# A decoder layer on one core: indexer queries for tokens 128 to 511 only, and the forgetting bias as causal strips loaded per query block

## The chip, the core and the metric

The kernel runs on one core of a Trainium2 chip. The metric is the device time of one execution in microseconds (us); lower is better. The kernel before takes 1047.29 us (median of 3 runs, 1047.10 to 1047.31).

The core has five engines that run their own instruction streams in order and wait for each other through semaphores: PE (TensorE, matrix products into PSUM), DVE (VectorE), ACT (ScalarE), POOL (GpSimd) and SP (SyncE, which here only issues DMAs). In the profile PEld is PE's loading of weights, which runs beside its matmuls.

## The reference, cut to what matters

One decoder layer for 512 tokens of width 1024: a half-step feed-forward block, a mixing stage, a second half-step feed-forward block. The mixing stage projects the normalised tokens `h` and runs two attentions of 8 heads of width 64 each, in blocks of 128 queries. The change touches two places in it.

```
# branch A, forgetting attention: log_f per token and head
cum = cumsum(log_f over tokens)
logits[t,s] = q_t.k_s / 8 + cum[t] - cum[s]       for s <= t, else -1e30
o_A = softmax(logits) @ v
...
# branch B, sparse attention: an indexer scores the keys, top 128 are kept
score[t,s] = sum over 8 heads of w[t,h] * relu(q_idx[t,h].k_idx[s] / 8)
score = where(s <= t, score, -1e30);  sel = top_k(score, 128)
o_B = softmax over sel of (q.k / 8 + rel_bias[bucket(t - s)]) @ v
```

Queries 0 to 127 can see at most 128 keys, so top-k keeps them all and their scores decide nothing. A softmax does not change when a number that depends on the query alone, such as `cum[t]`, is left out of its logits.

## The kernel before, in words

Everything is held with tokens or features on the 128 partitions; T = 512 tokens are NT = 4 blocks of 128. Matrix products are in split form: each operand is a high part plus a low part (`wh`, `wl` for weights, `xh`, `xl` for activations), and `mm3` (lines 154 to 157) issues three matmuls per product. A matmul of 128x512 reads 512 columns of the moving operand.

**Who sets the order.** PE's order is the order in which the program is written. All other engines and the DMA queues are ordered by a scheduler that places instructions by estimated times. SP issues nearly all loads in one in-order queue: the weight chunks (`load_w`, line 143, 512 KB each, three raw buffers `ra`, `rb`, `rc`), the key halves `kh`, `kl` (line 1300) and the bias tiles (line 1306).

**The filler.** The projections of the mixing stage are `units` (small columns `s`, indexer queries `iq0` to `iq3`, gates `ga`, keys, queries and values of branch A `fk`, `fq`, `fv`, queries of branch B `dq`, and so on), run by a generator. `prod.run(us)` runs filler steps until a budget is used up; each step yields its own estimate, `MM` = 0.64 for one feature-major step of three 128x512 matmuls, MM/2 for a token-major step of three 128x256 matmuls. `prod.finish(n)` runs units to the end whatever the budget.

**The indexer** (lines 1210 to 1226, 354 to 381 us). Units `iq0` to `iq3` each make the queries of two indexer heads (24 matmuls `ps_f`), and `stack_split` turns each into two tiles `st`: ACT copies the high part (line 916), DVE subtracts for the low part (line 917), tokens 0 to 511. For each of 8 heads and query blocks i = 1, 2, 3 there are two score matmuls `ps_ix` of 128x128(i+1), then ACT's relu (line 1220) and DVE's weighted sum into `sc` (line 1224). Block 0 is never scored. The score matmuls alternate between two PSUM tags of two buffers each. Filler of 0.5 us budget lies ahead of each.

**Top-k** (lines 1183 to 1193). 16 rounds of a maximum (MAX8, line 1187) and a replacement (MATCH_REPLACE8, line 1189) on each of three `sc` tiles, and three last comparisons (line 1192): 99 steps on DVE. They are handed out by `topk_run`: 1.25 steps per 0.64 us of filler after the indexer until the unit `fq0` is done, then for 30 further rounds, and after that two steps per attention block. DVE also splits the weights (line 150), the queries and keys (lines 920, 890).

**The running sums.** `forget()` makes `cum` on PE and DVE, `ncum` = -`cum` on DVE (line 1174), transposes `cum`, and stores it in DRAM as `cum_rows` (line 1181).

**The attention loop** (lines 1374 to 1400, 432 to 645 us). Heads g = 0 to 7 are branch A, 8 to 15 branch B. For each head s = 0 to 3 handles query block i = 3 - s. `softmax_block` (from line 1231):

- POOL makes the bias tile `b` for the block. For g < 8 that is a TENSOR_SCALAR `b<-cb,ncum` (line 1312: `cb` is one row of `cum_rows` read into all 128 partitions, and `ncum` a number per query) and an AFFINE_SELECT on the diagonal 128x128 (line 1313), which puts BIG above the diagonal. For g >= 8 it is one TENSOR_TENSOR (line 1316).
- PE makes the scores `ps_qk` (two PSUM buffers), DVE adds `b` and takes the minimum of each row in one instruction (line 1238, `p<-ps_qk,b`), ACT takes the exponential with its row sum (line 1240), DVE the reciprocal `rs` (line 1241), POOL the scaling `p<-p,rs` (line 1242).

`value_step` follows one head later: PE transposes the four `p` tiles (`pt`, line 1249), ACT and DVE split the result into `ph`, `pl` (lines 1253, 1254), and PE multiplies them with the values (`po`, lines 1259 and 1260). `get_bias(g + 1)` issues the DMA for the next head's `cb` at s = 0; `cb` has two buffers. Filler runs inside every block.

Of the kernel before, what the change touches and what calls it, by code (L numbers as in the profile page):

```python
# [12 lines left out]
F32 = mybir.dt.float32  # L13
# [42 lines left out]
def tile_hybrid_layer(ctx: ExitStack, tc: tile.TileContext, a: dict):  # L56
# [812 lines left out]
    with (tc.tile_pool(name="mix", bufs=1) as mp, ExitStack() as att_ctx,  # L869
# [6 lines left out]
        sg = at.tile([P, NT, S_W - 128], F32, name="sg")  # L876
# [4 lines left out]
        cum = at.tile([P, NT, H], F32, name="cum")  # L881
        ncum = at.tile([P, NT, H], F32, name="ncum")
# [26 lines left out]
        def stack_split(ps, g, nm):  # L909

            out = []
            for hf in range(2):
                own, oth = slice(hf * DH, hf * DH + DH), slice(DH - hf * DH, P - hf * DH)
                st = at.tile([P, T], F32R, tag=nm[hf], bufs=2, name="st")
                if g is None:
                    S.copy(st[own], ps[own])
                    V.tensor_sub(st[oth], ps[own], st[own].bitcast(F32))
                else:
                    S.mul(st[own], ps[own], g[own])
                    V.scalar_tensor_tensor(st[oth], ps[own], g[own], st[own].bitcast(F32),  # L920
                                           op0=OP.mult, op1=OP.subtract)
                out.append(st)
            return out
# [9 lines left out]
        def fm_proj(w, moving, kn, done):  # L933
            def run():
                ps = acc_tile("ps_f")
                wh, wl = w()
                for k in range(kn):
                    mm3(ps, wh[:, k], wl[:, k], moving[0][k], moving[1][k], k == 0, k == kn - 1)
                    if k < kn - 1:
                        yield MM  # L940
                done(ps)
                yield MM
            return run
# [128 lines left out]
        for c in range(4):  # L1072
            unit(f"iq{c}", fm_proj(weight(a["w_iq"][c], KD, P), (xh, xl), KD, iq_done))
# [71 lines left out]
        def forget():  # L1145
# [26 lines left out]
            PE.matmul(pc[:, :NT * H], ones, before.rearrange("p t h -> p (t h)"), start=False, stop=True)  # L1172
            V.tensor_copy(cum, pc[:, :NT * H].rearrange("p (t h) -> p t h", t=NT))
            V.tensor_scalar(ncum, cum, -1.0, None, op0=OP.mult)
# [128 lines left out]

        def get_bias(g):
            cb = at.tile([P, T], F32, tag="cb", bufs=2, name="cb")
            nc.sync.dma_start(cb, cum_rows[g:g + 1, :].to_broadcast([P, T]) if g < H else a["rel"][g - H])

            def bias(i):
                n = P * (i + 1)
                b = tmp_tile("b")  # L1310
                if g < H:
                    G.tensor_scalar(b[:, :n], cb[:, :n], 1.0, ncum[:, i, g:g + 1], op0=OP.mult, op1=OP.add)
                    G.affine_select(out=b[:, i * P:n], in_=b[:, i * P:n], compare_op=OP.is_ge, fill=BIG, base=0,
                                    pattern=[[-1, P]], channel_multiplier=1)
                else:
                    G.tensor_sub(b[:, :n], sc[i] if i else cpos, cb[:, T - n:T])
                return b[:, :n]
            return bias
# [6 lines left out]
        for step in range(30):  # L1325
# [8 lines left out]
            if step == 24:  # L1334
                nb = get_bias(0)
# [38 lines left out]
        for g in range(2 * H):  # L1374
            q, k, bias = nq, nk, nb
            probs[g] = [None] * NT
            st = [small.tile([P, NT], F32, tag=nm, name=nm) for nm in ("mn", "rs")]
            for s in range(NT):
# [6 lines left out]
                if g + 1 < 2 * H:  # L1385
                    if s == 0:
                        nb = get_bias(g + 1)
                    if s == 0 and g % 2:
                        nk = get_k(g + 1)
                    if s == 1 and g % 2:  # L1390
                        nq = get_q(g + 1)
# [131 lines left out]
```

## Time and profile before

| | |
|---|---|
| median of 3 runs | 1047.29 us (1047.10 to 1047.31) |
| the profiled execution, its own time | 1047.09 us |
| span of its trace | 1045.4 us |
| mean granted TensorE clock | 0.999 |
| PE busy | 1033.6 us, 99% of the span |
| DVE busy | 852.9 us, 82% |
| ACT busy | 669.0 us, 64% |
| POOL busy | 259.3 us, 25% |
| DMA | 142.66 MB, mean 136 GB/s |

How to read it: the span runs from the first to the last instruction in the trace; 1.7 us of the execution lie around it. A matmul's busy time overlaps with its neighbours', so the pace of a run of matmuls is read from their starts. In a timeline, a number in brackets is the engine's idle time just before, and behind the arrow stands what ended it. "waited for" rows give the total, the number of times and the longest.

### The profile page before, as it was taken

How to read it: one execution, taken by the hardware profiler on the slowest of the kernel's cores; microseconds unless marked ns; L12 is line 12 of the kernel's file. 1: busy time of each engine (PE TensorE's matmuls, PEld its weight loads, DVE VectorE, ACT ScalarE, POOL GpSimd, SP SyncE). 2: the span in 40 equal slices, each digit the busy share in tenths (PEclk: the TensorE clock that was granted, in tenths of full speed). 3: DMA queues.
4: the chain of work that ended last, by engine and by line, in shares of the span. 5: the costliest groups of instructions: out<-in, count | busy, mean ns of one | idle time of the engine just before them, and what ended most of it. 6: DMA issues, size and time to landing. Idle time of an engine off the chain costs nothing.

```text
span 1045.4 us, 19485 instructions
## 1 busy us (share of the span) xinstructions
PE 1033.6 (99%) x7424; PEld 962.6 (92%) x7424; DVE 852.9 (82%) x1405; ACT 669.0 (64%) x1118; POOL 259.3 (25%) x324
## 2 busy tenths in 40 slices
PE   9999999999999999999999999999999999999998
PEld 8889999999999898989977788888889999999998
DVE  6897888897989689977778765854887888988887
ACT  6547765865777766567867665433735865775773
POOL 1100111120121024386977653000100210111111
PEclk9999999999999999999999999999999999999999
DMA  7444765666567358633324321532553666567554
GB/s 259 105 151 120 158 165 129 152 163 173 120 150 182 91 147 192 188 104 90 92 69 117 117 70 51 158 131 74 131 168 90 152 147 182 127 160 190 135 127 131
DMA packets 57341, 142.66 MB, mean 136 GB/s; under 512 B 6424, under 2 KB 15768, under 8 KB 57248
## 3 DMA queue, kind: packets, MB, share of 16 engines
q1 hardware_dynamic: 39600, 110.21, 34.7%
q0 software_dynamic: 17504, 30.94, 16.5%
q8 instruction: 58, 0.95, 0.4%
q10 hardware_dynamic: 144, 0.27, 0.1%
q14 instruction: 35, 0.29, 0.1%
HBM read 104.94 MB, written 3.42 MB: 104 GB/s over the span
## 4 chain that ended last, share of the span: by engine, by line
PE 86%; DVE 9%; POOL 2%; issue 2%; ACT 1%; DVEq 0%; POOLq 0%; ACTq 0%
PE pB L157 5%; PE pB L156 5%; PE pB L155 5%; PE pA L157 3%; PE pA L155 3%; PE pA L156 3%; PE ps_f L155 3%; PE ps_f L156 3%; PE ps_f L157 3%; PE dB L157 2%; PE dB L155 2%; PE dB L156 2%; DVE sc L1189 2%; DVE m L1187 2%; PE dA L156 2%
## 5 line engine op out<-in xcount | busy, mean ns | idle before, releaser
L123 ACT CAST wh<-s 128x1024 fp32r<-128x1024 f32 (+1 forms) x90 | 86.7, 963 | 66.1 <-PE pC L156 31.6
L130 DVE TENSOR_TENSOR wl<-s,wh 128x1024 fp32r<-128x1024 f32 (+1 forms) x90 | 100.2, 1113 | 20.0 <-ACT wh L123 20.0
L155 PE MATMUL ps_t<-wh,xh 128*128 128x256 f32 (+1 forms) x288 | 81.1, 282 | 0.0
L156 PE MATMUL ps_t<-wl,xh 128*128 128x256 f32 (+1 forms) x288 | 80.2, 279 | 0.0
L157 PE MATMUL ps_t<-wh,xl 128*128 128x256 f32 (+1 forms) x288 | 80.2, 279 | 0.0
L155 PE MATMUL pB<-tbh,wh 128*128 128x256 f32 x288 | 79.5, 276 | 0.0
L156 PE MATMUL pB<-tbl,wh 128*128 128x256 f32 x288 | 79.5, 276 | 0.0
L157 PE MATMUL pB<-tbh,wl 128*128 128x256 f32 x288 | 79.5, 276 | 0.0
L249 POOL DMA_DIRECT2D b<-gu x12 | 10.4, 864 | 220.4 <-DVE rb L449 89.4
L155 PE MATMUL ps_f<-xh,wh 128*128 128x512 f32 x152 | 60.8, 400 | 0.0
L157 PE MATMUL ps_f<-xh,wl 128*128 128x512 f32 x152 | 59.6, 392 | 0.0
L156 PE MATMUL ps_f<-xl,wh 128*128 128x512 f32 x152 | 59.6, 392 | 0.0
L1240 ACT ACTIVATE p<-p,mn 128x512 f32<-128x512 f32 (+1 forms) x64 | 36.0, 562 | 30.8 <-DVE mn L1238 30.5
L155 PEld LDWEIGHTS ps_t<-wh,xh 128*128 128x128 f32 x288 | 54.4, 189 | 0.4
L156 PEld LDWEIGHTS ps_t<-wl,xh 128*128 128x128 f32 x288 | 54.4, 189 | 0.4
L157 PEld LDWEIGHTS ps_t<-wh,xl 128*128 128x128 f32 x288 | 54.4, 189 | 0.0
L157 PEld LDWEIGHTS pB<-tbh,wl 128*128 128x128 f32 x288 | 54.1, 188 | 0.0
L155 PEld LDWEIGHTS pB<-tbh,wh 128*128 128x128 f32 x288 | 54.1, 188 | 0.0
L156 PEld LDWEIGHTS pB<-tbl,wh 128*128 128x128 f32 x288 | 54.1, 188 | 0.0
L575 POOL DMA_DIRECT2D gx<-e x20 | 23.9, 1241 | 119.6 <-ACT wh L123 99.9
L1242 POOL TENSOR_SCALAR p<-p,rs 128x512 f32<-128x512 f32 (+1 forms) x64 | 39.1, 614 | 57.8 <-DVE rs L1241 53.8
L1254 DVE TENSOR_TENSOR pl<-pt,ph 128x512 fp32r<-128x512 f32 (+1 forms) x64 | 31.0, 484 | 19.6 <-ACT ph L1253 19.4
(406 smaller groups left out, 4195.1 us busy)
## 6 DMA issues: line engine op xcount, KB each, us to landing
rf<-in_w_pair_dram SPq DMA_DIRECT2D x15, 512.0 KB, 4.1
rc<-in_w_pair_dram SPq DMA_DIRECT2D x12, 512.0 KB, 3.6
re<-in_w_pair_dram SPq DMA_DIRECT2D x12, 512.0 KB, 3.6
rd<-in_w_pair_dram SPq DMA_DIRECT2D x12, 512.0 KB, 3.9
rb<-in_w_pair_dram SPq DMA_DIRECT2D x12, 512.0 KB, 4.2
gx<-e POOLq DMA_DIRECT2D x22, 256.0 KB, 4.2
ra<-in_w_pair_dram SPq DMA_DIRECT2D x9, 512.0 KB, 3.5
rd<-in_w_halves_dram SPq DMA_DIRECT2D x12, 384.0 KB, 3.7
```

The costliest lines, as they stand in the source:

```text
L123: S.copy(wh[:, :f], raw[:, :f])
L130: V.tensor_sub(wl[:, :f], raw[:, :f], wh[:, :f].bitcast(F32))
L155: PE.matmul(out, lh, rh, start=start, stop=False, **more)
L156: PE.matmul(out, lh, rl, start=False, stop=False, **more)
L157: PE.matmul(out, ll, rh, start=False, stop=stop, **more)
L249: G.dma_start(l, src, accum_op=OP.add)
L575: G.dma_start(xa[:, d:d + 2, HT:], t["e"][part], accum_op=OP.add)
L1187: V.max(m8, sc[i])
L1189: V.match_replace(out=sc[i], in_to_replace=m8, in_values=sc[i], imm_value=-3e38)
L1240: S.activation(p, p, AF.Exp, bias=mn, scale=-1.0, accum_out=rs)
L1242: G.tensor_scalar(p, p, rs, 1.0, op0=OP.mult, op1=OP.mult)
L1254: V.tensor_sub(pl[:, sl], pt[:, sl], ph[:, sl].bitcast(F32))
```

## The change

Two edits, in one program.

**Indexer queries.** The units `iq0` to `iq3` run `fm_proj` with `begin` = 128: their 96 matmuls have 384 columns instead of 512, each filler step yields 0.48 instead of 0.64, and `stack_split` copies and subtracts columns 128 to 511 only. Tokens 0 to 127 of these tiles, which nothing reads, stay unwritten.

**Forgetting bias.** `cum[t]` is dropped from the logits, so `ncum` and POOL's TENSOR_SCALAR (line 1312 before) go. For each head and block a strip of `cum_rows` of just 128(i+1) columns is loaded by its own DMA, AFFINE_SELECT masks the diagonal in place in the strip, and DVE reads the strip itself. So there are four DMAs a head instead of one (640 KB instead of 256 KB written). Strips 3 and 2 have one `cb` buffer each in turn; strips 1 and 0 share one tile in the place of `sg`. A strip of head g + 1 can be loaded only when head g's strip in that place has been read: strip 3 after the DVE instruction of block 3, strip 2 after block 2, strips 1 and 0 after block 0.

```diff
-        sg = at.tile([P, NT, S_W - 128], F32, name="sg")
+        sg = at.tile([P, 3 * P], F32, tag="sg", name="sg")[:, :NT * (S_W - 128)].rearrange("p (t c) -> p t c", t=NT)
...
-                    S.copy(st[own], ps[own])
-                    V.tensor_sub(st[oth], ps[own], st[own].bitcast(F32))
+                    S.copy(st[own, P:], ps[own, P:])
+                    V.tensor_sub(st[oth, P:], ps[own, P:], st[own, P:].bitcast(F32))
...
-        def fm_proj(w, moving, kn, done):
+        def fm_proj(w, moving, kn, done, begin=0):
...
+                us = MM * (T - begin) / T
                 for k in range(kn):
-                    mm3(ps, wh[:, k], wl[:, k], moving[0][k], moving[1][k], k == 0, k == kn - 1)
+                    mm3(ps[:, begin:], wh[:, k], wl[:, k], moving[0][k][:, begin:], moving[1][k][:, begin:],
+                        k == 0, k == kn - 1)
...
-            unit(f"iq{c}", fm_proj(weight(a["w_iq"][c], KD, P), (xh, xl), KD, iq_done))
+            unit(f"iq{c}", fm_proj(weight(a["w_iq"][c], KD, P), (xh, xl), KD, iq_done, P))
...
-            V.tensor_scalar(ncum, cum, -1.0, None, op0=OP.mult)
...
+        def causal_rows(g, i):
+            if i:
+                strip = at.tile([P, T] if i > 1 else [P, 3 * P], F32, tag="cb" if i > 1 else "sg",
+                                bufs=2 if i > 1 else 1, name="cb")
+            else:
+                strip = strips[1][:, 2 * P:]
+            n = P * (i + 1)
+            nc.sync.dma_start(strip[:, :n], cum_rows[g:g + 1, :n].to_broadcast([P, n]))
+            G.affine_select(out=strip[:, i * P:n], in_=strip[:, i * P:n], compare_op=OP.is_ge, fill=BIG, base=0,
+                            pattern=[[-1, P]], channel_multiplier=1)
+            strips[i] = strip
...
-                if g < H:
-                    G.tensor_scalar(b[:, :n], cb[:, :n], 1.0, ncum[:, i, g:g + 1], op0=OP.mult, op1=OP.add)
-                    G.affine_select(out=b[:, i * P:n], in_=b[:, i * P:n], compare_op=OP.is_ge, fill=BIG, base=0,
-                                    pattern=[[-1, P]], channel_multiplier=1)
-                else:
-                    G.tensor_sub(b[:, :n], sc[i] if i else cpos, cb[:, T - n:T])
+                G.tensor_sub(b[:, :n], sc[i] if i else cpos, cb[:, T - n:T])
...
-                nb = get_bias(0)
+                for i in (3, 2, 1, 0):
+                    causal_rows(0, i)
...
-            q, k, bias = nq, nk, nb
+            q, k, bias = nq, nk, forget_bias if g < H else nb
...
-                    if s == 0:
+                    if g + 1 < H:
+                        for i in ((3,), (2,), (), (1, 0))[s]:
+                            causal_rows(g + 1, i)
+                    elif s == 0:
                         nb = get_bias(g + 1)
```

**How instructions move.** On POOL, at the start of the attention loop, before (`b` the bias tiles of heads 0 and 1, `p` the scaled probabilities of head 0):

```order
78 L1312 TENSOR_SCALAR b<-cb,ncum 128x512
79 L1312 TENSOR_SCALAR b<-cb,ncum 128x384
80 L1312 TENSOR_SCALAR b<-cb,ncum 128x256
81 L1312 TENSOR_SCALAR b<-cb,ncum 128x128
82 L1313 AFFINE_SELECT b<-b 128x128 x4
83 L1242 TENSOR_SCALAR p<-p,rs 128x512
84 L1312 TENSOR_SCALAR b<-cb,ncum 128x512
85 L1313 AFFINE_SELECT b<-b 128x128
86 L1242 TENSOR_SCALAR p<-p,rs 128x384
87 L1242 TENSOR_SCALAR p<-p,rs 128x256
88 L1242 TENSOR_SCALAR p<-p,rs 128x128
```

The five TENSOR_SCALARs seen here, and the 27 behind them, are gone in the changed kernel; the selects stay. The same place on POOL in the changed kernel (`cb` is now a strip; the fifth select of the first row and those between the `p` rows are on head 1's strips):

```order
78 L1312 AFFINE_SELECT cb<-cb 128x128 x5
79 L1242 TENSOR_SCALAR p<-p,rs 128x512
80 L1312 AFFINE_SELECT cb<-cb 128x128
81 L1242 TENSOR_SCALAR p<-p,rs 128x384
82 L1242 TENSOR_SCALAR p<-p,rs 128x256
83 L1312 AFFINE_SELECT cb<-cb 128x128 x2
84 L1242 TENSOR_SCALAR p<-p,rs 128x128
```

Before, no select of the next head stands ahead of a `p` with a wait of its own for a DMA that this head's blocks release; now the selects on head 1's strips 3, 2, and 1 with 0 stand ahead of head 0's `p` of blocks 3, 2 and 0. Selects on strips 1 and 0 stand ahead of the last `p` of a head in heads 0, 1 and 5.

On DVE, around the top-k's last steps, before (the fifth `p,mn<-ps_qk` of the loop, block 3 of head 1, and what is near it):

```order
567 L1187 MAX m_5525<-sc_4155 128x8
568 L897 TENSOR_REDUCE ss<-sqh 128x8
569 L1192 TENSOR_SCALAR sc_4153<-sc_4153 128x256
570 L1238 ISA p,mn<-ps_qk,b 128x512
571 L1238 ISA mn 128x1
572 L1241 RECIPROCAL rs<-rs 128x1
573 L1192 TENSOR_SCALAR sc_4154<-sc_4154 128x384
```

The first two of the three last comparisons (line 1192) lie on both sides of head 1's block 3. The last steps of the top-k on DVE in the changed kernel (here the `p,mn` is that of head 1's block 1):

```order
588 L1254 TENSOR_TENSOR pl<-pt,ph 128x384
589 L1238 ISA p,mn<-ps_qk,cb 128x256
590 L1238 ISA mn 128x1
591 L1192 TENSOR_SCALAR sc_4151<-sc_4151 128x256
592 L1192 TENSOR_SCALAR sc_4152<-sc_4152 128x384
593 L918 SCALAR_TENSOR_TENSOR st<-ps_q,gq,st 64x512
594 L1238 ISA p,mn<-ps_qk,cb 128x128
```

The top-k ends two blocks later in the order: ahead of the first `p,mn` of the loop stand 78 top-k steps where 85 stood, because the indexer's filler, now shorter by step, reaches further into the units and fewer rounds of the loop that hands out top-k steps are left.

More of the change, by code (lines that the diff above doesn't have):

```diff
@@ L880, in tile_hybrid_layer @@
         dvv = at.tile([P, NT, P], F32R, name="dvv")
-        cum = at.tile([P, NT, H], F32, name="cum")
-        ncum = at.tile([P, NT, H], F32, name="ncum")
         dram = att_ctx.enter_context(tc.tile_pool(name="dram", bufs=1, space=bass.MemoryType.DRAM))
@@ L936, in run @@
                 wh, wl = w()
+                us = MM * (T - begin) / T
                 for k in range(kn):
-                    mm3(ps, wh[:, k], wl[:, k], moving[0][k], moving[1][k], k == 0, k == kn - 1)
+                    mm3(ps[:, begin:], wh[:, k], wl[:, k], moving[0][k][:, begin:], moving[1][k][:, begin:],
+                        k == 0, k == kn - 1)
                     if k < kn - 1:
-                        yield MM
+                        yield us
                 done(ps)
-                yield MM
+                yield us
             return run
@@ L1172, in forget @@
             PE.matmul(pc[:, :NT * H], ones, before.rearrange("p t h -> p (t h)"), start=False, stop=True)
+            cum = small.tile([P, NT, H], F32, tag="cr", bufs=1, name="cum")
             V.tensor_copy(cum, pc[:, :NT * H].rearrange("p (t h) -> p t h", t=NT))
-            V.tensor_scalar(ncum, cum, -1.0, None, op0=OP.mult)
             yield
@@ L1302, in get_k, with forget_bias @@
             return out
+        def causal_rows(g, i):
[9 more added lines that the diff above has]
+            strips[i] = strip
+        strips = {}
+        def forget_bias(i):
+            return strips[i][:, :P * (i + 1)]
         def get_bias(g):
             cb = at.tile([P, T], F32, tag="cb", bufs=2, name="cb")
-            nc.sync.dma_start(cb, cum_rows[g:g + 1, :].to_broadcast([P, T]) if g < H else a["rel"][g - H])
+            nc.sync.dma_start(cb, a["rel"][g - H])
             def bias(i):
```

## The prediction

> **What bounds the kernel now.** I began with the page: busy times, then the chain that ended last.
>
> ```profile
> PE 1033.6 (99%) x7424; PEld 962.6 (92%) x7424; DVE 852.9 (82%) x1405; ACT 669.0 (64%) x1118; POOL 259.3 (25%) x324
> PE 86%; DVE 9%; POOL 2%; issue 2%; ACT 1%; DVEq 0%; POOLq 0%; ACTq 0%
> ```
>
> PE is busy for 99% of the span and holds 86% of the chain. So work taken from PE's stream shortens the kernel, unless another engine then makes PE wait. DVE's 9% of the chain has to sit somewhere, so next I read the stages that the change touches by windows (us, then busy time of PE, PEld, DVE, ACT, POOL).
>
> ```profile
> 354.60:381.00 26.40, 26.40 (x129) 22.43 (x129) 19.58 (x40) 20.24 (x37) 2.73 (x4) 1.00 0.44 105
> 381.00:432.00 51.00, 51.00 (x375) 47.76 (x375) 50.55 (x147) 27.94 (x44) 20.30 (x21) 1.00 0.77 191
> 432.00:460.00 28.00, 25.94 (x211) 25.12 (x211) 26.49 (x74) 18.22 (x38) 17.52 (x25) 1.00 0.49 147
> 460.00:480.00 20.00, 18.26 (x148) 17.49 (x146) 13.21 (x30) 13.76 (x31) 17.45 (x27) 1.00 0.28 84
> 480.00:537.00 57.00, 55.52 (x394) 50.95 (x393) 44.43 (x107) 44.35 (x102) 44.58 (x67) 1.00 0.32 86
> ```
>
> In the indexer (354.6 to 381) PE never stops and DVE has 6.8 us free. From 381 to 432, the top-k, DVE is full: 50.55 of 51. In the heads of branch A (432 to 537) PE loses 2.06 + 1.74 + 1.48 = 5.3 us; the waits of PE over the whole run say for whom.
>
> ```profile
> PE pt L1249 <- POOL p L1242: 3.1, 3, 1.5
> PE po L1260 <- DVE pl L1254: 2.2, 3, 0.8
> PE ps_qk L928 <- DVE mn L1238: 0.9, 2, 0.6
> ```
>
> Nowhere does PE wait for a DMA or a weight. The change can gain by less PE work (the indexer's queries) and by shorter waits in branch A; it can lose by making full DVE or POOL late.
>
> **Term A, the narrow matmuls: -5.0 us.** The pace is read from starts: the 4th and the 27th matmul of the indexer's queries, with 22 of the same kind between; then two score matmuls of 384 columns and the matmul behind them; and the weight loads of a large group.
>
> ```profile
> 344.18 0.40 PE L155 MATMUL ps_f<-xh,wh 128*128 128x512 f32 x1
> 349.42 0.39 PE L157 MATMUL ps_f<-xh,wl 128*128 128x512 f32 x1
> ...
> 354.90 0.34 PE L928 MATMUL ps_ix<-ikh,st 128*128 128x384 f32 x1
> 355.08 0.34 PE L929 MATMUL ps_ix<-ikl,st 128*128 128x384 f32 x1
> 355.25 0.39 PE L155 MATMUL ps_f<-xh,wh 128*128 128x512 f32 x1
> ...
> L155 PEld LDWEIGHTS ps_t<-wh,xh 128*128 128x128 f32 x288 | 54.4, 189 | 0.4
> ```
>
> 5.24 us over 23 steps is 0.228 us for 512 columns; 0.35 over two is 0.175 for 384. 96 matmuls x 0.053 = 5.0 us, all of it on PE, which does not stop there. The weights are loaded as often as before; a load is shown with 0.189 us, but the score matmuls keep 0.175 with a load each, so loads overlap and do not set this pace.
>
> A rule of the Trainium skill speaks against this size: TensorE: Matmul & The Clock Gate, section Back-to-back issue gap, gives for a sustained stream of weight load and matmul some 81 ns at 128 columns and 131 ns at 512. By it 128 columns less are worth (131 - 81) / 3 = 17 ns, or 1.6 us for 96. The trace disagrees with it at 512 columns, 228 ns; it is a rival below.
>
> **Term B, ACT at the indexer's start: +0.3 us (0 to 1.6).** PE comes to the first scores about 1.5 us earlier: the first unit is 24 x 0.053 = 1.3 us shorter, and the steps behind it a little. ACT has the same work ahead of them.
>
> ```profile
> 351.49 1.28 ACT L1156 ACT_TABLE_LOAD   x1
> 355.10 0.84 ACT L1220 ACTIVATE relu<-ps_ix 128x256 f32<-128x256 f32 x2 [0.92 <-PE ps_ix L929]
> 355.92 1.05 ACT L144 CAST wh<-rc 128x1024 fp32r<-128x1024 f32 x1
> ```
>
> Before, the first relu waited 0.92 us for PE; an ACT that does not get faster uses up 1.5 - 0.9 = 0.6 us. The table load (1.28) stays ahead of that relu, and in the new order so does the weight cast (1.05) that stood behind it: 1.6 us with nothing covered. Four PSUM buffers lie between score matmuls and relu, so PE meets the delay only at the fifth block, and I take 0.3. After that ACT has 6 of 26 us free, and loses work: eight copies get narrower.
>
> **Term C, DVE and the top-k: +1.0 us (0 to 2.4).** The order puts 78 top-k steps ahead of the first softmax minimum instead of 85; these seven come back before head 1's block 0.
>
> ```profile
> L1189 DVE MATCH_REPLACE8 sc<-m,sc 128x256 f32<-128x256 f32 (+2 forms) x48 | 25.6, 538 | 0.0
> L1187 DVE MAX8 m<-sc 128x8 f32<-128x384 f32 (+2 forms) x47 | 24.0, 547 | 0.1
> L150 DVE TENSOR_TENSOR wl<-ra,wh 128x1024 fp32r<-128x1024 f32 x2 | 2.4, 1208 | 0.0
> ...
> L1224 DVE SCALAR_TENSOR_TENSOR sc<-relu,wi,sc 128x512 f32<-128x512 f32 x6 | 4.5, 750 | 2.1 <-ACT relu L1220 2.1
> L1224 DVE SCALAR_TENSOR_TENSOR sc<-relu,wi,sc 128x384 f32<-128x384 f32 x7 | 4.3, 613 | 1.0 <-ACT relu L1220 0.9
> ...
> L1174 DVE TENSOR_SCALAR ncum<-cum x1: 1504/1504/1504, 412.5 to 412.5; 128x32 f32<-128x32 f32 x1
> ```
>
> DVE saves eight times 128 columns of a subtract, 750 - 613 = 0.137 us each by the nearest rows, 1.1 us, and `ncum`, 1.5 us: 2.6 us. Up to the first softmax it also has 7 x 0.54 = 3.8 us of top-k less, 6.4 in all against PE's 5.0, so it is no worse placed than before. When the seven steps have come back, in head 1, it is 5.0 - 2.6 = 2.4 us short of PE's lead. What PE needs of it there is the low part `pl` of head 0:
>
> ```profile
> 458.58 0.42 DVE L1254 TENSOR_TENSOR pl<-pt,ph 128x256 fp32r<-128x256 f32 x1
> ...
> 460.01 0.28 PE L1260 MATMUL po<-pl,fv 128*128 128x256 f32 x1
> ```
>
> That has 460.01 - 459.00 = 1.0 us to spare: 1.4 is left, and as DVE is not quite full in its window (26.49 of 28) I take 1.0. With no spare it is 2.4. From 460 on DVE has 6.8 of 20 us free and catches up.
>
> **Term D, POOL without its TENSOR_SCALARs: -0.9 us (0 to -3.2).**
>
> ```profile
> L1312 POOL TENSOR_SCALAR b<-cb,ncum 128x512 f32<-128x512 f32 (+3 forms) x32 | 21.6, 684 | 10.1 <-DMA cb<-cum_rows 10.1
> DVE p L1238 <- POOL b L1313: 2.2, 5, 0.6
> ```
>
> 21.6 of POOL's 79.6 us between 432 and 537 go, and with them five waits of DVE for a bias, 2.2 us; what PE can gain is only what it waits for itself.
>
> ```profile
> 474.53 2.34 DVE L150 TENSOR_TENSOR wl<-rb,wh 128x1024 fp32r<-128x1024 f32 x1
> ...
> 474.75 1.04 POOL L1002 TENSOR_TENSOR kn<-kn,rh 128x512 f32<-128x512 f32 x1
> ...
> 477.24 1.04 POOL L1242 TENSOR_SCALAR p<-p,rs 128x128 f32<-128x128 f32 x2 [1.45 <-DVE rs L1241]
> ...
> 477.67 0.55 PE L1249 MATMUL pt<-ident,p 128*128 128x128 f32 x3 [1.40 <-POOL p L1242]
> ```
>
> Here a weight split of DVE took 2.34 us instead of 1.21 while POOL ran, the reciprocals stood behind it, POOL waited 1.45 us for them, and PE 1.40 for POOL's `p`. In a less crowded POOL some of such meetings end: I take half of this wait and 0.2 of the smaller ones. The lower bound gives back all 3.1 us of the first PE wait row, and 0.1 beside.
>
> The Trainium skill (SBUF — State Buffer, section Who interferes with whom) says that a DVE instruction with two SBUF inputs and a GpSimd instruction that reads SBUF shut each other out for a whole instruction. The row agrees: the excess, 1.13 us, is about the one `kn` of 1.04. That `kn` stays, so by this rule the gain here could as well be nothing.
>
> **Term E, selects that wait for a strip: +0.7 us (0 to 8.4).** The new wait is the heart of the second edit: SP may issue the next head's strip only when DVE has read this head's, and behind that strip POOL's select, and behind the select the `p` of this head, are in line.
>
> ```profile
> cb<-cum_rows SPq DMA_DIRECT2D x8, 256.0 KB, 4.3
> ...
> 445.18 0.27 DVE L1238 CUSTOM_DVE_ANT_0 p<-ps_qk,b 128x128 f32<-128x128 f32 x1
> ...
> 448.28 0.40 POOL L1242 TENSOR_SCALAR p<-p,rs 128x128 f32<-128x128 f32 x1 [1.57 <-DVE rs L1241]
> ...
> 444.22 0.33 SPq L143 DMA_DIRECT2D ra<-in_w_dq_dram  x1
> ...
> L1313 POOL TENSOR_SCALAR_AFFINE_SELECT b<-b 128x128 f32<-128x128 f32 x32 | 9.2, 306 | 0.3
> ```
>
> Head 0's last `p` started 2.8 us after its minimum was done (445.45). The strip's way is two issues of 0.33, a landing of 4.3 at 256 KB (the strips here have 128 and 64 KB, whose landing no row shows; I let it go down to 3) and two selects of 0.31: 4.3 to 5.6 us. So this `p` comes 1.5 to 2.8 us later, in the three heads (0, 1, 5) where the order has these selects ahead of a head's last `p`; 3 x 2.8 = 8.4 is the far bound. PE needs that `p` only a block later, with filler between, and by its row of waits it waited for a `p` just three times. I take half of 1.5, in one head.
>
> SP's other work behind the waiting strips is weight loads and key halves. For instance strip 2 of head 1 waits for the minimum below and stands ahead of the load at 444.22 above.
>
> ```profile
> 440.33 0.55 DVE L1238 CUSTOM_DVE_ANT_0 p<-ps_qk,b 128x384 f32<-128x384 f32 x1
> ```
>
> The load was issued 3.3 us after this minimum ended, for reasons of its own. Price nothing; without that cover a load would come one issue, 0.33 us, later per strip. The 384 KB more per head (640 instead of 256) meet DMA engines that are 0.28 to 0.49 busy: nothing.
>
> **The sum.** -5.0 + 0.3 + 1.0 - 0.9 + 0.7 = -3.9 us. The profiled execution took 1047.09 (span 1045.4 and 1.7 around it), 0.2 below the median 1047.29; from 1047.1 the forecast is 1043.2 us.
>
> **The rivals.**
>
> *DVE keeps the gain.* If PE is held by a full DVE from the top-k on, and the weight splits stay stretched, C is at its 2.4, B at 1.6 and D nothing: -5.0 + 1.6 + 2.4 + 0.7 = -0.3, 1046.8. For it: 50.55 of 51 us. Against it: DVE's own list gets 2.6 us shorter and it is idle a third of the time from 460. Chance 0.12.
>
> *POOL waits for strips, slower.* E at 8.4 with D nothing: -5.0 + 0.3 + 1.0 + 8.4 = +4.7, 1051.8. It decides (over 2.1 us slower) from E = 5.8, 1.9 us in each of the three heads, which is a landing of 2.8 + 1.9 - 0.7 - 0.6 = 3.4 us with no filler of PE in between. For it: 4.3 us in the row above, and DMA traffic that grows. Against it: smaller strips, and `pt` a block behind `p`. Chance 0.06.
>
> *Columns do not set the pace.* The stream is held by its weight loads, which stay, and A is nothing; then PE has no lead, and B and C vanish too: -0.9 + 0.7 = -0.2, 1046.9. Against it: score matmuls at 0.175, with a weight load each. Chance 0.03. By the Trainium skill's section named above, with 1.6 us for A, it would be -1.8, 1045.3.
>
> *Branch A's waits go as well.* B, C and E nothing and D at -3.2: -8.2, 1038.9. For it: POOL at 17.45 of 20 us where PE waits. Against it: two of the `p` waits end with DVE's reciprocal. Chance 0.09.
>
> **How the numbers follow.** My forecast, some 1041 to 1045, has 0.70. Over 0.2% (2.1 us, about what a measurement of this kernel can tell from no change) means below 1045.2 or above 1049.4. Faster: 0.70, 0.08 of the last rival, and a little of the DVE case, 0.80. Slower: 0.05. The rest, 0.15, is within. The range 1040.0 to 1046.0 leaves out the slow rival, the deepest gain and half of the DVE case.
>
> **What would show each step.** The loop of heads now begins here:
>
> ```profile
> 432.61 0.39 PE L928 MATMUL ps_qk<-kh,st 128*128 128x512 f32 x1
> ```
>
> A: starts of `ps_f` 0.175 us apart in the indexer's queries, first `ps_qk` at about 428 us instead of 432.6. B: an idle PE near 357 us, or none. C: the wait of `po` for `pl` in head 0's values, 1 us more. D: no bias waits on DVE, and the wait of `pt` for `p` below 3.1 us in all. E: POOL idle for a DMA into `cb` ahead of a `p`. After head 7 all should run as before, earlier by the sum. I am wrong if A's pace is not there, or if PE's idle time between 430 and 537 leaves 5.3 us by more than 2 either way.

## The result, and the profile after

The changed kernel takes 1053.07 us (median of 6 runs, 1050.58 to 1055.49); the kernel before, run beside it, 1047.19 us (6 runs, 1046.59 to 1047.65). The ratio is 1.0057 with a 95% interval of 1.0044 to 1.0070: slower by 5.9 us, where 3.9 us less had been forecast. The profiled execution took 1050.58 us (span 1048.9) and is the quickest of the six, with a mean granted clock of 0.997 where the six have 0.992 to 0.997, so its trace, 3.5 us above that of the kernel before, shows less than the whole 5.9 us.

The page of the changed kernel, busy times and then the chain of work that ended last:

```profile
PE 1029.5 (98%) x7424; PEld 963.2 (92%) x7424; DVE 848.3 (81%) x1404; ACT 668.8 (64%) x1118; POOL 240.3 (23%) x292
PE 87%; DVE 7%; DMA 3%; issue 1%; ACT 1%; SPq 0%; POOL 0%; POOLq 0%; DVEq 0%; ACTq 0%
```

PE (1033.6 before), DVE (852.9) and POOL (259.3) have less work. New is the second line's DMA with 3% of the chain; before, no DMA stood in it. The windows of the same stages (time of PE, PEld, DVE, ACT, POOL, then the granted clock, DMA share, GB/s):

```profile
381.00:432.00 51.00, 51.00 (x370) 47.71 (x369) 48.12 (x139) 24.84 (x36) 20.19 (x22) 1.00 0.73 181
432.00:460.00 28.00, 20.67 (x154) 20.09 (x153) 23.70 (x67) 17.61 (x37) 11.38 (x16) 0.88 0.43 141
...
480.00:537.00 57.00, 52.06 (x379) 48.20 (x378) 42.65 (x101) 43.38 (x96) 33.41 (x45) 1.00 0.40 117
```

Up to 432 PE does not stop. In the heads of branch A it loses 7.33 us between 432 and 460 and 4.94 between 480 and 537, where it had lost 2.06 and 1.48 (between 460 and 480 it loses 0.68 instead of 1.74); and in the first of these stretches the granted clock is 0.88 instead of 1.00. For whom PE and POOL waited:

```profile
PE pt L1249 <- POOL p L1242: 8.6, 3, 5.0
PE ps_qk L926 <- DVE mn L1238: 2.3, 1, 2.3
...
POOL cb L1312 <- DMA cb<-cum_rows: 46.7, 20, 10.1
```

20 selects waited for their strip, 46.7 us together; most of that hurts nobody. What does hurt is seen in the timeline (SP's rows are issues; the brackets give the idle time before and what ended it):

```profile
343.08 0.34 PE L156 MATMUL ps_f<-xl,wh 128*128 128x384 f32 x1
...
346.89 0.33 PE L157 MATMUL ps_f<-xh,wl 128*128 128x384 f32 x1
...
420.64 0.82 SPq L1311 DMA_DIRECT2D cb<-cum_rows  x2
...
421.99 0.95 SPq L1311 DMA_DIRECT2D cb<-cum_rows  x2
...
423.05 0.43 SPq L143 DMA_DIRECT2D rc<-in_w_fq_dram  x1
...
427.10 0.39 PE L926 MATMUL ps_qk<-kh,st 128*128 128x512 f32 x1
...
432.42 1.05 ACT L144 CAST wh<-rc 128x1024 fp32r<-128x1024 f32 x1 [7.71 <-DMA rc<-in_w_fq_dram]
...
433.50 1.23 DVE L150 TENSOR_TENSOR wl<-rc,wh 128x1024 fp32r<-128x1024 f32 x1 [4.13 <-ACT wh L144]
...
437.56 0.33 PE L926 MATMUL ps_qk<-kh,st 128*128 128x128 f32 x1 [2.35 <-DVE mn L1238]
...
441.99 0.28 DVE L1238 CUSTOM_DVE_ANT_0 p<-ps_qk,cb 128x128 f32<-128x128 f32 x1
...
442.30 1.98 SPq L1311 DMA_DIRECT2D cb<-cum_rows  x3
...
443.51 0.28 PE L157 MATMUL ps_t<-wh,xl 128*128 128x256 f32 x1
...
447.45 0.91 POOL L1312 TENSOR_SCALAR_AFFINE_SELECT cb<-cb 128x128 f32<-128x128 f32 x2 [4.13 <-DMA cb<-cum_rows]
...
448.35 0.37 POOL L1242 TENSOR_SCALAR p<-p,rs 128x128 f32<-128x128 f32 x1
...
448.77 1.12 PE L1249 MATMUL pt<-ident,p 128*128 128x128 f32 x4 [4.98 <-POOL p L1242]
...
465.02 0.66 PE L1249 MATMUL pt<-ident,p 128*128 128x128 f32 x4 [0.68 <-POOL p L1242]
...
519.47 0.66 PE L1249 MATMUL pt<-ident,p 128*128 128x128 f32 x4 [2.98 <-POOL p L1242]
```

The first two rows, with 21 of their kind between, give the pace of the narrow matmuls: 0.173 us. In the rows below them the loss has two places. **The queue:** head 0's four strips (the first two and second two rows) stand ahead of the weight load `rc` on SP. It is issued at 423.05 and its cast starts at 432.42; ACT had stood 7.71 us for it, DVE 4.13 us for ACT, the minimum of head 0's block 2 stands in DVE's order behind the split, and PE waited 2.35 us for it. **The select:** the minimum of head 0's block 0 is done at 442.27; then strips 1 and 0 of head 1 may be loaded, their selects run at 447.45, and only behind them in POOL's order the `p` of head 0. PE came to it at 443.79 and stood 4.98 us. The same happens at the ends of heads 1 (465.02, 0.68 us) and 5 (519.47, 2.98 us). What followed the long wait shows in windows of 2 us:

```profile
444.00:446.00 2.00, 0.00 (x0) 0.00 (x0) 2.00 (x7) 2.00 (x6) 0.00 (x0) 1.00 0.57 126
446.00:448.00 2.00, 0.00 (x0) 0.00 (x0) 2.00 (x5) 0.27 (x1) 0.55 (x1) 0.56 0.61 194
448.00:450.00 2.00, 1.23 (x5) 1.23 (x6) 0.88 (x4) 0.07 (x1) 2.00 (x5) 0.50 0.68 208
450.00:452.00 2.00, 2.00 (x10) 2.00 (x10) 1.34 (x4) 1.20 (x2) 1.92 (x3) 0.50 0.33 121
452.00:454.00 2.00, 2.00 (x15) 2.00 (x14) 1.92 (x5) 0.71 (x2) 0.40 (x1) 0.73 0.41 107
```

PE idles to 448.77, and the clock then stays at 0.50 to about 453.2: 4.4 us of work at half speed are, as an estimate, another 2.2 us. The Trainium skill (TensorE: Matmul & The Clock Gate, section HAM oscillation — how this bites in real kernels) says that a wait which crosses the clock monitor's window puts PE back to half rate. The trace agrees for the wait of 4.98 us; behind the waits of 2.35 and 2.98 us the clock stayed at 1.00.

### The profile page after: what moved, and what is told of

It is laid out like the page before. It is cut to its first block, busy times and chain, and to the rows that moved or that the text cites. A ratio compares the mean times of both kernels' runs of the same rounds, so it can differ in the third digit from the quotient of the medians.

```text
span 1048.9 us, 19502 instructions
## 1 busy us (share of the span) xinstructions
PE 1029.5 (98%) x7424; PEld 963.2 (92%) x7424; DVE 848.3 (81%) x1404; ACT 668.8 (64%) x1118; POOL 240.3 (23%) x292
## 4 chain that ended last, share of the span: by engine, by line
PE 87%; DVE 7%; DMA 3%; issue 1%; ACT 1%; SPq 0%; POOL 0%; POOLq 0%; DVEq 0%; ACTq 0%
PE pB L155 5%; PE pB L156 5%; PE pB L157 5%; PE pA L155 3%; PE pA L156 3%; PE pA L157 3%; PE ps_f L155 3%; PE ps_f L157 3%; PE ps_f L156 3%; PE dB L157 2%; PE dB L155 2%; PE dB L156 2%; PE dA L156 2%; PE dA L155 2%; DVE sc L1189 2%; PE pC L155 2%
## 5 line engine op out<-in xcount | busy, mean ns | idle before, releaser
L155 PE MATMUL ps_f<-xh,wh 128*128 128x512 f32 (+1 forms) x152 | 59.0, 388 | 0.0
L157 PE MATMUL ps_f<-xh,wl 128*128 128x512 f32 (+1 forms) x152 | 57.8, 381 | 0.0
L156 PE MATMUL ps_f<-xl,wh 128*128 128x512 f32 (+1 forms) x152 | 57.7, 380 | 0.0
```

The costliest lines, as they stand in the source:

```text
L155: PE.matmul(out, lh, rh, start=start, stop=False, **more)
L156: PE.matmul(out, lh, rl, start=False, stop=False, **more)
L157: PE.matmul(out, ll, rh, start=False, stop=stop, **more)
```

## The experiments

The theory after the result: the query edit keeps its gain, and the strips cost more than it, by the weight load behind them on SP and by the selects ahead of `p`. The rivals: the earlier indexer makes a full DVE late (so the query edit is the cause); the selects do not matter and only the queue does, or the other way round; and, as the runs went on, that 128 partitions reading one row of DRAM is the root of both. All times are medians; "against before" is the difference to the median of before measured beside it.

| run | us | ratio to before, 95% | against before, us |
|---|---|---|---|
| the changed kernel | 1053.07 | 1.0057 (1.0044 to 1.0070) | +5.9 |
| e1_queries | 1043.56 | 0.9969 (0.9957 to 0.9980) | -3.1 |
| e2_strips | 1059.99 | 1.0119 (1.0103 to 1.0135) | +13.4 |
| e3_selects_late | 1047.56 | 1.0007 (0.9998 to 1.0016) | +0.9 |
| e4_row_per_partition | 1042.71 | 0.9966 (0.9953 to 0.9979) | -4.1 |
| e5_act_queue | 1047.95 | 1.0010 (1.0001 to 1.0019) | +1.3 |
| e6_late_and_act | 1045.20 | 0.9985 (0.9976 to 0.9994) | -1.6 |
| e7_one_row | 1045.05 | 0.9983 (0.9974 to 0.9992) | -1.7 |
| e8_idle_strips | 1071.39 | 1.0230 (1.0213 to 1.0247) | +24.6 |
| e9_copies | 1044.62 | 0.9977 (0.9969 to 0.9986) | -2.3 |
| e10_query_copies | 1043.84 | 0.9973 (0.9964 to 0.9981) | -3.1 |
| e11_late_copies | 1042.58 | 0.9964 (0.9951 to 0.9978) | -4.3 |
| e12_keep_busy | 1051.85 | 1.0039 (1.0025 to 1.0053) | +4.8 |
| e13_store_copies_read_one | 1048.36 | 1.0016 (1.0007 to 1.0024) | +1.5 |
| e14_copies_strips_first | 1051.68 | 1.0050 (1.0036 to 1.0063) | +4.9 |
| e15_late_rc_first | 1042.98 | 0.9962 (0.9949 to 0.9974) | -3.8 |

### One edit at a time

e1_queries is the kernel before with the diff's lines on `fm_proj`, `stack_split` and `iq` alone; e2_strips is the changed kernel without them:

```diff
-            unit(f"iq{c}", fm_proj(weight(a["w_iq"][c], KD, P), (xh, xl), KD, iq_done, P))
+            unit(f"iq{c}", fm_proj(weight(a["w_iq"][c], KD, P), (xh, xl), KD, iq_done))
```

> The narrower query matmuls alone, the forgetting bias as in the kernel before. If the strips are what costs, this kernel keeps term A and is 4 to 5 us faster than before: 1042 to 1043.5 us, granted clock 0.999, the first ps_qk of the loop near 427 us, and no 4 us wait of DVE for a weight cast near 430. If the loss comes from the earlier indexer (PE now ahead of a full DVE, the top-k steps later), it is 1046 us or more, with waits of PE for mn or pl near 440 to 460 as in the changed kernel.

> The strips alone, the queries with 512 columns as before. If the strips are what costs, this kernel is slower than before by about what the changed kernel lost plus what term A gave, 8 to 12 us: 1055 to 1059 us, with a granted clock below 0.998 and POOL idle some 40 us for strips. If the loss comes from the earlier indexer, it is within 2 us of before, 1045 to 1049 us.

Measured: -3.1 and +13.4 us. The rival of the earlier indexer falls: with the old bias the query edit is a gain, with the old indexer the strips are a loss. The gain is a microsecond under what was expected; PE's waits in e1_queries say where that went:

```profile
PE po L1262 <- DVE pl L1256: 2.8, 4, 0.8
...
PE pt L1251 <- DVE pl L1256: 1.9, 2, 1.2
```

PE waits 4.7 us for `pl` (2.8 and 1.9), before 2.2; the other waits are shorter. The strips cost 13.4 us with the old indexer and 9.0 with the new one (from -3.1 to +5.9). No run parts these two, but the trace of e2_strips shows where most of the difference can lie: PE waits 3.17 us for a minimum and 3.12 and 3.60 us for a `p`, and behind each of the three the granted clock falls to 0.50. Estimated by windows of 0.5 us, that costs PE some 6 us, where the one such stretch in the trace of the changed kernel costs 2.2.

### The selects, and the queue

e3_selects_late puts each select behind the last `p` of the head before:

```diff
-            G.tensor_scalar(p, p, rs, 1.0, op0=OP.mult, op1=OP.mult)
+            scaled = G.tensor_scalar(p, p, rs, 1.0, op0=OP.mult, op1=OP.mult)
+            if i == 0:
+                head_end[0] = scaled
...
         def forget_bias(i):
+            with tc.issue_after(head_end[0].ins) if head_end[0] else nullcontext():
+                G.affine_select(out=strip[:, i * P:n], in_=strip[:, i * P:n], compare_op=OP.is_ge, fill=BIG, base=0,
+                                pattern=[[-1, P]], channel_multiplier=1)
```

e5_act_queue issues the strips from ACT instead of SP, and e6_late_and_act does both:

```diff
-            nc.sync.dma_start(strip[:, :n], cum_rows[g:g + 1, :n].to_broadcast([P, n]))
+            nc.scalar.dma_start(strip[:, :n], cum_rows[g:g + 1, :n].to_broadcast([P, n]))
```

> Both edits, but each select is put behind the last p of the head before, so that no p stands behind a select that waits for a strip. If the place of the selects on POOL is the main cost, the wait of pt for p falls from 8.6 us to below 3, the granted clock stays at 0.999, and the time falls by 4 us or more, to 1049 us or less; the price could be that the first minimum of a head now waits for its select, up to 1 us a head. If the loads queued behind strips, or the strips' landing by itself, are the main cost, the time stays within 1.5 us of the changed kernel, 1051.5 to 1054.5 us.

> Both edits, the strips issued by ACT's DMA queue instead of SP's, so that no weight load stands behind a strip in a queue. If the queue is a main cost, the 4.1 us wait of DVE for a weight cast near 430 us falls below 1.5 us and the time falls by 2 us or more, to 1051 us or less. If the selects ahead of p are the main cost, the wait of pt for p stays at 6 us or more and the time within 1.5 us of 1053.1 us. If the strips slow the weight loads through the DMA engines that they share, and not through the queue, the wait of DVE for that cast also stays.

> Both edits, with the selects put behind the last p of the head before and the strips issued by ACT's DMA queue. Each of the two alone took 5.5 and 5.1 us off the changed kernel's 1053.1. If they are two separate costs, they add up: 1042.5 us (1041.5 to 1044.5), as good as the query edit alone, with the wait of pt for p below 2 us and no 4 us wait of DVE near 430. If both end the same idle stretch and what follows from it, the second adds little: 1046.5 to 1048.5 us.

Each alone takes some 5 us off, so neither "only the queue" nor "only the selects" holds. In e3_selects_late the cast of `rc` still starts as late as 433.30, and PE waits 2.7 us for a minimum there; in e5_act_queue `rc`, now issued ahead of the strips (420.44), lands after 4.0 us instead of 9.3, but PE waits 7.1 us for `p`. Together they give -1.6, where the sum of the two would be +5.9 - 5.0 - 4.6 = -3.7; what ACT's queue takes back there was not tried (PE waits 1.6 us for a `p` and 1.1 us for a minimum in that trace). The Trainium skill (DMA: Bandwidth & Descriptors, section Issuing engines are not separate DMA queues) says that another issuing engine saves only the time of the issue, as all share the same DMA engines. The 4.6 us of e5_act_queue go beyond that, but the load's place explains them: e15_late_rc_first, below, gets as much on SP's own queue.

### Is reading one row 128 times the root?

e4_row_per_partition reads each strip from 128 rows of the table of relative biases (so the strips hold other numbers than the running sums, and head 0's do not wait for `cum_rows`). e9_copies keeps the running sums 16 times in DRAM; e10_query_copies and e11_late_copies do that to e1_queries and e3_selects_late:

```diff
-        cum_rows = dram.tile([H, T], F32, name="cum_rows")
+        cum_rows = dram.tile([COPIES, H, T], F32, name="cum_rows")
...
-            nc.sync.dma_start(cum_rows, cum_t)
+            nc.sync.dma_start(cum_rows.rearrange("c h t -> h c t"), cum_t[:, None, :].to_broadcast([H, COPIES, T]))
...
-            nc.sync.dma_start(strip[:, :n], cum_rows[g:g + 1, :n].to_broadcast([P, n]))
+            nc.sync.dma_start(strip[:, :n], cum_rows[:, g:g + 1, :n].to_broadcast([COPIES, P // COPIES, n]))
```

> Both edits, but a strip is read from 128 different rows of another table instead of one row for all partitions (the bias has other numbers, and head 0's strips need not wait for the running sums). If reading one row 128 times is what makes a strip land late, 2.5 us or more and 3.6 in the middle, the landings fall well below 2.5 us and the time to 1049 us or less. If the place of the selects and the queue decide, the landings are alike and the time within 2 us of 1053.1 us, less what head 0's strips gain by coming earlier (the wait near 430, up to 3 us).

> The changed kernel, with the running sums stored 16 times in DRAM and each strip read from all 16 copies, 8 partitions to a copy, instead of 128 partitions from one row. Order, queue, waits and sizes are those of the changed kernel; only where the bytes are read differs. If reading one row 128 times is what makes the strips land late and holds up the loads beside them, the landings of 64 and 128 KB fall from 4.4 and 3.6 us to 2.6 or less, the weight load that took 9.3 us takes 6 or less, and the time is 1042 to 1045 us. If the run with a row per partition gained because head 0's strips came before the crowded stretch, or if the place of the selects and the queue cost by themselves, it is 1050 us or more.

> The query edit alone, its one row per head read from the 16 copies. If the reading of one row 128 times costs the kernel of before too (its weight loads beside it took 5.6 and 6.7 us), this is 1 us or more faster than the query edit alone at 1043.56: 1042.5 us or less. If its loads are hidden anyway, it is 1043 to 1044 us.

> Both edits, the selects behind the last p of the head before, the strips read from the 16 copies by SP's queue. If the reading was the root and the place of the selects only let it through to PE, this is no better than the copies alone: within 1 us of that run. If the place of the selects costs by itself, a microsecond or more better than the copies alone, 1043 us or less.

Two of the four times came out as the reading theory has them, e4 and e9. The other two did not: e10 is no faster than e1_queries, and e11 is 2.0 us below e9 where the theory had them within 1 us (their intervals overlap). Nor did the landings of e9 (the last number is the median us from issue to landing). The changed kernel:

```profile
cb<-cum_rows SPq DMA_DIRECT2D x8, 256.0 KB, 3.6
...
cb<-cum_rows SPq DMA_DIRECT2D x8, 128.0 KB, 3.6
...
rc<-in_w_fq_dram SPq DMA_DIRECT2D x1, 512.0 KB, 9.3
cb<-cum_rows SPq DMA_DIRECT2D x8, 64.0 KB, 4.4
```

With 16 copies:

```profile
cb<-cum_rows SPq DMA_DIRECT2D x8, 256.0 KB, 3.8
...
cb<-cum_rows SPq DMA_DIRECT2D x8, 128.0 KB, 2.8
...
rc<-in_w_fq_dram SPq DMA_DIRECT2D x1, 512.0 KB, 6.6
cb<-cum_rows SPq DMA_DIRECT2D x8, 64.0 KB, 3.7
```

A row per partition (heads 1 to 7):

```profile
cb<-in_rel_dram SPq DMA_DIRECT2D x7, 128.0 KB, 2.4
cb<-in_rel_dram SPq DMA_DIRECT2D x7, 64.0 KB, 2.0
```

The row per partition lands sooner, 2.0 us for 64 KB against 4.4 (in this trace a select that waits for a strip stands ahead of a `kn` on POOL before the loop, and PE waits 4.1 us for a `kn`). The copies do so by less than 1 us for the two small strips, and not for 256 KB (3.6 and 3.8) or 192 KB (3.4 and 4.2). And the expectation for the copies was wrong on one point: the order was not that of the changed kernel. With the larger store `rc` is issued at 420.00, ahead of head 0's strips. Three more kernels part the two: e13 stores 16 copies but reads only the first, e14 reads 16 copies but puts `rc` back behind the strips, e15 is e3_selects_late with head 0's strips written three filler steps later, so that `rc` stands behind strip 3 alone, with one row and one store.

```diff
-            nc.sync.dma_start(strip[:, :n], cum_rows[:, g:g + 1, :n].to_broadcast([COPIES, P // COPIES, n]))
+            nc.sync.dma_start(strip[:, :n], cum_rows[0, g:g + 1, :n].to_broadcast([P, n]))
...
+            with tc.issue_after(strip_load.pop().ins) if strip_load else nullcontext():
+                nc.sync.dma_start(raw[:, :f].rearrange("p (n m) -> p n m", n=n), src)
...
-            if step == 24:
+            if step == 27:
```

> The kernel of the copies, but each strip is read from the first copy alone, one row for 128 partitions; the 16-fold store stays, and with it the order on SP, in which the weight load rc of the queries stands ahead of head 0's strips (in the changed kernel it stood behind all four). If the copies made the 8.5 us, this kernel is back at 1049 us or more. If that order made it, it is 1043.5 to 1046 us, as the copies were at 1044.62.

> The kernel of the copies, with the weight load rc put back behind head 0's four strips on SP, as in the changed kernel. If the copies made the 8.5 us, it stays at 1043.5 to 1046 us and rc lands within 6 us. If the order made it, it is 1049 us or more, rc lands after 8 us or more, and DVE waits 3 us or more for its cast near 430.

> The kernel with late selects, with head 0's strips written three filler steps later, so that on SP the weight load rc stands behind strip 3 alone and ahead of strips 2, 1 and 0; one row, one store. If that order is what the late selects still lacked, it falls from 1047.56 to 1042.5 to 1044.5 us, and the wait of ps_qk for mn, 2.7 us, goes. If it was the reading of one row, it stays at 1046.5 us or more.

e14 is back at +4.9: with `rc` behind the strips the copies do not mend the kernel. It is no clean measure of the copies, as the larger store also delays head 0's strips, from 420.64 to 424.01 us, and `rc` behind them. PE's waits for `p` fall from 8.6 to 3.2 us, but its wait for the minimum behind `rc` grows from 2.3 to 5.2. e13 is at +1.5, between the two answers that had been written down: the order is worth 4.4 us (from +5.9; e13 has the larger store too), and copies on top of it 3.8 more. e15 needs no copies: -3.8, the order being worth 4.7 from e3_selects_late's +0.9, and the late selects 5.3 from e13. Its timeline near `rc`, and its waits for `pl`:

```profile
421.56 0.35 SPq L1313 DMA_DIRECT2D cb<-cum_rows  x1
...
422.00 0.38 SPq L143 DMA_DIRECT2D rc<-in_w_fq_dram  x1
...
422.97 1.70 SPq L1313 DMA_DIRECT2D cb<-cum_rows  x3
...
428.07 1.05 ACT L144 CAST wh<-rc 128x1024 fp32r<-128x1024 f32 x1 [2.54 <-PE ps_t L157]
...
430.12 1.22 DVE L150 TENSOR_TENSOR wl<-rc,wh 128x1024 fp32r<-128x1024 f32 x1
```

```profile
PE pt L1251 <- DVE pl L1256: 3.9, 4, 2.0
PE po L1262 <- DVE pl L1256: 3.6, 7, 1.0
```

The cast waits for PE's own buffer and no longer for its load, DVE goes from the minimum straight to the split, and PE's waits for `p` and for a minimum are gone; what is left in the loop are waits for `pl`, 7.5 us. So 128 readers of one row are not the root: e15 has them still. They lengthen a landing, and that counts where selects stand ahead of `p` and `rc` ahead of the strips (e13 to e9, 3.8 us); with the selects late it is 0.5 us (e15 to e11), within the intervals, and e10 shows nothing on the query edit.

### Other ways, and the clock

e7_one_row has no strips: one row per head, loaded a head ahead, with the diagonal masked in that row itself, one block after the other. e8_idle_strips is e1_queries with the strips' loads added into a tile that nobody reads. e12_keep_busy puts 16 idle matmuls ahead of head 0's first transposes.

```diff
+                if g < H:
+                    with tc.issue_after(scaled[-2].ins) if len(scaled) > 1 else nullcontext():
+                        G.affine_select(out=cb[:, i * P:n], in_=cb[:, i * P:n], compare_op=OP.is_ge, fill=BIG, base=0,
+                                        pattern=[[-1, P]], channel_multiplier=1)
+                    return cb[:, :n]
...
+                nc.sync.dma_start(strip[:, :n], cum_rows[g:g + 1, :n].to_broadcast([P, n]))
...
+            if keep:
+                for _ in range(16):
+                    PE.matmul(pt, keep[0][:, :P], keep[0], start=True, stop=True)
```

> Both edits without strips: one row per head, loaded by one DMA a head ahead as before, and each block's select masks the diagonal in that row itself, so it waits for the minimum of the block before, not for a DMA, and the order puts it behind the p of the block before that. The TENSOR_SCALARs and ncum are gone. If freeing POOL gives the 0.9 us of term D, it is 1042.7 us (1041.5 to 1043.2), faster than the query edit alone at 1043.56. If it gives nothing, it is 1043.2 to 1044.2. If a minimum that waits for a select costs PE (4 blocks of 8 heads, each about 0.4 us of POOL and its signal in DVE's way), it is over 1045.

> The query edit alone, and beside the one row per head three more loads of 384, 256 and 128 columns at the places of the strips, into a tile that nobody reads: the traffic and the queue places of the strips without any wait of POOL or DVE for them. If the added traffic holds up the weight loads, DVE waits 2 us or more for a weight cast near 430 and the time is 1045.5 us or more. If only the waits for buffers and strips cost, it is 1043 to 1044.5 us, as the query edit alone.

> The changed kernel with 16 extra matmuls of 128x512 (some 3.7 us by the pace of 0.228 us) on PE just ahead of head 0's first transposes, where PE stood 5.0 us for a p and the granted clock then fell to 0.50; their result is overwritten by the transposes. If the standstill is what lowers the clock, the clock stays at 1.00 from 444 to 456 us, the matmuls behind keep 0.11 us at 128x256 instead of 0.21, and the time falls by the 2.2 us that 4.4 us at half speed cost: 1049.5 to 1052 us. If the clock falls for another reason, the dip stays and the time is 1052.5 to 1054.5 us.

e7 gives -1.7, less than the query edit alone. It has no DMA wait ahead of `p`; instead one wait of 4.5 us for the `p` of head 0, in front of which POOL's new order has a 1.67 us `rh` and a 2.31 us `kn`. Behind that wait the granted clock is 0.50 from 446 to 452, which costs an estimated 2.9 us (by windows of 0.5 us). So e7 does not show what a freer POOL is worth.

e8 did not test what it was meant to: with one buffer for the idle tile, each of its loads waits on SP until the one before it has landed. It shows instead what a queue costs that waits. PE's two largest waits there:

```profile
PE pt L1254 <- DVE pl L1259: 13.2, 3, 11.3
PE ps_qk L926 <- DMA kh<-kh: 8.5, 1, 8.5
```

The key halves stood behind loads that nobody needed, and so did a bias row that was needed: POOL waited 12.7 us for it, DVE for POOL, and PE 11.3 us for a `pl` behind that in DVE's order. The run is at +24.6 us against before, 27.7 against the query edit. Whether the strips' traffic costs by itself stays open.

e12 keeps the clock, as these windows show (two of those of the changed kernel above, then a later one):

```profile
446.00:448.00 2.00, 2.00 (x10) 1.68 (x9) 2.00 (x8) 1.48 (x5) 0.42 (x1) 1.00 0.59 181
448.00:450.00 2.00, 0.65 (x4) 0.24 (x3) 2.00 (x6) 0.47 (x1) 2.00 (x5) 1.00 0.64 159
...
520.00:530.00 10.00, 9.73 (x56) 8.66 (x54) 7.24 (x16) 7.33 (x17) 6.40 (x7) 0.87 0.14 47
```

Without the standstill the clock does not fall there. It falls at another, unfilled one: PE's longest wait for `p` in this run is 3.5 us, and the clock is 0.87 behind 520, which takes back an estimated 1.6 us (by windows of 0.5 us). The time came down by 1.1 us, within the range written down, but the intervals of the two ratios overlap: the trace shows the mechanism, the time does not settle its price.

## Why the prediction was wrong

**Term A** was right in its pace: in the changed kernel the query matmuls start 0.173 us apart (343.08 to 346.89 in 22 steps; 0.175 forecast), and PE waits for nothing up to 432. The first `ps_qk` comes at 427.10 where "about 428" was written.

**Term B** is nothing: there is no wait of PE between 340 and 432.

**Term C** lies at its far end. In e1_queries, which has the narrow queries alone, PE waits 2.5 us longer for `pl` than before, where 1.0 was taken and 2.4 was the bound. The three new waits (1.16, 0.71 and 0.59 us) lie at head 0's values, where the prediction had put the cost. With them the query edit keeps 5.0 - 2.5 = 2.5 us; it gives 3.1, as PE's other waits got about 1 us shorter, and the interval (2.1 to 4.5 us) covers the rest.

**Term D** shows no more than 0.7 us: e15_late_rc_first, where neither `p` nor a weight load waits for a strip, is that much better than e1_queries, and their intervals overlap. Its `p` waits are gone altogether (3.1 us before), as the far end had it, but PE's waits for `pl` have grown from 4.7 us in e1_queries to 7.5.

**Term E is the step that failed.** It was priced at 0.7 us and is worth 9.0 (from -3.1 to +5.9). The prediction's own sign shows it: PE idles 7.33 + 0.68 + 4.94 = 12.95 us between 432 and 537, where 5.3 us, give or take 2, had been forecast. Three things in the term did not hold.

- "PE needs that `p` only a block later, with filler between": PE was at head 0's transposes 1.5 us after the minimum, and the `p` came 6.1 us after it instead of 2.8. The kernel before already showed how little cover there is: in its row below PE came to these transposes at 448.73 - 1.48 = 447.25, 1.8 us after the minimum that ended at 445.45, and waited.

```profile
448.73 0.66 PE L1249 MATMUL pt<-ident,p 128*128 128x128 f32 x4 [1.48 <-POOL p L1242]
```

The three heads were named rightly, 0, 1 and 5, and the waits there, 4.98 + 0.68 + 2.98 = 8.6 us, lie at the far bound of 8.4. In the time it is less: late selects take back 5.0 us (the changed kernel to e3) or 5.3 (e13 to e15), as PE then waits longer for `pl` (7.5 us in e3, 3.3 in the changed kernel). The landing, which was let go down to 3 us for the small strips, is 3.6 and 4.4.

- "Price nothing" for the loads behind strips. The instance looked at was a strip within the loop. The costly ones are the first four, issued together just before the loop, when `cum_rows` is ready: the weight load behind them landed 9.3 us after its issue, and the order on SP is worth 4.4 to 4.7 us.
- A wait was priced at its own length. One of 5 us on PE also halved the clock for the next 4.4 us, which this trace puts at 2.2 us. These lie within the two amounts above.

The two causes add up: from +5.9, less 4.4 for the order and 5.0 for the selects, -3.5 would be left, and e15 with both mended measures -3.8. That is near the -3.9 of the forecast, but for a kernel without the two waits, and in part by luck, as term C was taken at 1.0 and is 2.5. The rival with the right sign had 6 chances in 100 and put 1051.8. That it came near is luck too: it priced the selects alone at 8.4, where they are worth 5.0 to 5.3, and had nothing for the queue.

## What to carry to other kernels

A load that an engine is made to wait for costs in two places: on its own queue, for whatever is issued behind it, and on the engine, for whatever stands behind the instruction that needs it. Price each at the first use, where nothing has been loaded ahead, and not only at an instance in the steady loop. Look how long before its use an engine's result is ready, and compare that with the whole way of the wait put ahead of it. Of the two edits the narrow queries are worth keeping; the strips stop costing only with the weight load ahead of three of them and the selects behind `p`, and are then no measurable gain (e15, 1042.98 us, beats both kernels; against the query edit alone at 1043.56 the intervals do not tell them apart).

## What the runs showed of the hardware that had not been expected

Head 0's strips, 256, 192, 128 and 64 KB in this order, on POOL in the changed kernel:

```profile
424.40 1.04 POOL L1312 TENSOR_SCALAR_AFFINE_SELECT cb<-cb 128x128 f32<-128x128 f32 x1 [10.08 <-DMA cb<-cum_rows]
426.40 0.29 POOL L1312 TENSOR_SCALAR_AFFINE_SELECT cb<-cb 128x128 f32<-128x128 f32 x1 [0.96 <-DMA cb<-cum_rows]
428.29 0.29 POOL L1312 TENSOR_SCALAR_AFFINE_SELECT cb<-cb 128x128 f32<-128x128 f32 x1 [1.59 <-DMA cb<-cum_rows]
430.81 0.30 POOL L1312 TENSOR_SCALAR_AFFINE_SELECT cb<-cb 128x128 f32<-128x128 f32 x1 [2.23 <-DMA cb<-cum_rows]
```

They come 2.00, 1.89 and 2.52 us one after the other, the smallest last, and each select waits for its load: here the bytes did not set the time. One row read into 128 partitions landed in 4.4 us at 64 KB, 128 different rows in 2.0. By which part of the DMA path that comes is not settled.

How long PE may wait before the clock falls is not one number here. Behind waits of 2.91 us (e14), 3.12 and 3.17 (e2) and 3.48 (e12) the granted clock fell to 0.50; behind 2.94 (e12), 2.98 (the changed kernel) and 3.07 us (e13) it stayed at 1.00. Summed over windows of 0.5 us, the clock then stood at 0.50 for some 3.4 us (e9, e13) or for twice that (the changed kernel, e5, e7).
